# Rebuilt doors and attention in a two-layer trunk, with one of four weight homes given to the modulation

## The chip, the cores and the metric

The kernel runs on one core of a Trainium2 chip. The metric is the device time of one execution in microseconds (us); lower is better.

## What is computed

The reference is a decoder trunk of two layers on 256 rows of 2048 channels, all in float32. Each layer has a mixer and a feed-forward part (FFN), and both are wrapped in the same way:

```
mod = silu(c) @ w_ada[layer] + b_ada[layer]          # 6 x 2048 values: shift, scale, gate, twice
h = rmsnorm(x, g_pre) * (1 + sc) + sh
y = mixer(h)      # layer 0: gated MLP beside RWKV-7, one output projection; layer 1: attention
x = x + gt * rmsnorm(y, g_post)
h = rmsnorm(x, g_pre_ffn) * (1 + sc_f) + sh_f
gate, up = split(h @ w_ffn_in)                        # 2048 x 11264
x = x + gt_f * rmsnorm((silu(gate) * up) @ w_ffn_out, g_post_ffn)     # 5632 x 2048
```

With 256 rows the attention has a single key block, so each head is plain causal attention with a linear bias. The matrix `w_ada` is multiplied by one vector only.

## The kernel before

**Dense products.** `dense` computes 256 x 512 outputs: two row tiles of 128 (t = 0, 1), each summed in one PSUM bank `mm`. The weight comes in chunks of 2 x 128 rows by 512 columns, 512 KB each. `load_split` has SyncE (SP) load a chunk into a home `w32` (four of them in a ring, L193), ScalarE (ACT) round it to `wh` (L197) and VectorE (DVE) compute the rest `wl = w32 - wh` (L198); `wh` and `wl` have three buffers each. The activations are split in the same way into a high and a low part (`Ht`, `Lt`; named `hF`, `hFl` in the FFNs, `hA`, `hAl` in attention, `aH`, `aL` behind the gate). `mm_chunk` makes three products of 512 columns for each k tile and row tile (L209 high by `wh`, L210 high by `wl`, L211 low by `wh`), so 12 matmuls a chunk.

**Modulation.** The 320 blocks of `w_ada` that are worked off in the background are loaded by SP too (L150), 512 KB each, into homes of the tag `ada`, of which there are two. VectorE multiplies a block by the vector and sums it (L112), a "dot". Thirty-two dots make one of the ten vectors (0,2) to (1,5), finished at L136 to L143 (`mod`). After each chunk `pump` adds a rate to a credit and calls `ada_step` for each whole point: it issues a load and, as soon as as many are under way as there are homes, the dot of the oldest one.

**Order.** The program is written as one sequence and ordered by the framework's scheduler, per engine; `load_split` runs at a raised priority. Each engine works in order, and a waiting instruction holds up those behind it. SP's loads wait for a free home: a `w32` is free after its `wl`, an `ada` home after its dot.

**The doors.** Three times `residual_norm` leads from one part to the next: from layer 0's mixer to its FFN (door 1), from there to attention (door 2), from attention to layer 1's FFN (door 3). The last block of the part before is evacuated by `post_evac` (L261 `U`, L269 a sum, ACT squares), then the row sums are reduced (L284) and `X` is renewed block by block (L310, 512 columns and one row tile each). `X` is transposed by TensorE (L319), the second norm's factor is spread over all partitions by a small matmul (L327) and copied by ACT (L329); `h32` (tile `scr`, L338) multiplies transposed rows from PSUM by the scale and that factor, ACT adds the shift for `Ht` (L340), and VectorE gives `Lt` (L341). The scratch tiles take both homes of `ada`, after `ada_drain` has finished the dots under way.

**Attention.** Four groups of four heads. The three dense blocks of a group give k, q and v; k and q are copied (`znq`, L1152), transposed (L1159) and copied back. A generator (`Bg`) puts the heads of the group before between the chunks: scores (L1176, L1177), scale and bias, maximum, exponential, division (`pm`, L1190), transposes of `pm` (L1193), `pT`, and the product with v (L1199, L1200). Between these steps lie YA1, YA2 and YA3 points of credit, one point a chunk.

## Time and profile before

| what | us |
|---|---|
| median of three runs (lowest, highest) | 2522.0 (2519.48, 2523.02) |
| profiled execution, its span | 2523.41, 2521.7 |
| busy: TensorE | 2382.6 (94%) |
| busy: VectorE | 1668.5 (66%) |
| busy: ScalarE | 1078.7 (43%) |
| bytes loaded | 619.46 MB, 246 GB/s over the span |

The profile describes one execution; all its times count from the start of the span. "Busy" is time with an instruction under way on the engine; matmuls are pipelined, so a TensorE that is fed a little late still reads as busy. "PEclk" is the clock that TensorE was granted, as a share of 2.4 GHz.

By the trace the program runs so: start-up, gated MLP and RWKV to 553 us, the first FFN to 1337, attention with its output projection to 1752, the second FFN to 2511, the end of the output at 2521.7.

### The profile page before, as it was taken

The page shows a single profiled execution, that of the slowest core. Times are in us where ns is not written, and L with a number is a line of the kernel's source. Part 1 is how long each engine was busy: PE and PEld are TensorE (multiplying, and loading weights), DVE is VectorE, ACT ScalarE, POOL GpSimd, SP SyncE. Part 2 cuts the span into 40 slices and gives each one's busy share as a digit, 9 for nine tenths or more (in the row PEclk, how much of TensorE's full clock was granted, in tenths as well). Part 3 has the DMA queues.
Part 4 walks back from the last instruction along what each step waited for, and adds up shares of the span by engine and source line. Part 5 has one row for each costly group of instructions (what it writes and reads, how often), then busy time and mean ns, then how long its engine had stood idle before and what let it go on. Part 6 is the DMA issues. An engine that isn't in the chain of part 4 may idle for free. (4 is left out here: it accounts for less than half of the span.)

```text
span 2521.7 us, 30836 instructions
## 1 busy us (share of the span) xinstructions
PE 2382.6 (94%) x11536; PEld 1936.7 (77%) x11536; DVE 1668.5 (66%) x2267; ACT 1078.7 (43%) x1460; POOL 43.0 (2%) x30
## 2 busy tenths in 40 slices
PE   5898989978999999999998999999999999999998
PEld 4777877757877777888887777877777888888886
DVE  6759966888777777444447788876775544544444
ACT  2153444454444334444444444455444444444443
POOL 0001000000000000000000000100000000000000
PEclk9998989998999999999999999999999999999999
DMA  9975847786888888555555888975686555555554
GB/s 395 415 263 173 302 168 251 262 288 222 309 305 313 305 303 305 196 204 192 192 192 200 294 309 306 322 270 193 225 313 221 191 189 188 191 187 206 192 192 151
DMA packets 166566, 623.63 MB, mean 247 GB/s; under 512 B 18576, under 2 KB 18768, under 8 KB 161424
## 3 DMA queue, kind: packets, MB, share of 16 engines
q1 hardware_dynamic: 164256, 612.73, 69.0%
q10 hardware_dynamic: 2160, 8.94, 1.0%
q8 instruction: 90, 1.47, 0.2%
q14 instruction: 60, 0.49, 0.1%
HBM read 619.46 MB, written 2.13 MB: 246 GB/s over the span
## 5 line engine op out<-in xcount | busy, mean ns | idle before, releaser
L197 ACT ACTIVATE wh<-w 128x1024 fp32r<-128x1024 f32 x736 | 779.5, 1060 | 1087.1 <-PE mm L211 969.2
L198 DVE TENSOR_TENSOR wl<-w,wh 128x1024 fp32r<-128x1024 f32 x736 | 895.0, 1223 | 523.7 <-ACT wh L197 522.8
L210 PE MATMUL mm<-wl,hF 128*128 128x512 f32 x1408 | 554.8, 394 | 19.5 <-DVE wl L198 19.0
L209 PE MATMUL mm<-wh,hF 128*128 128x512 f32 x1408 | 553.4, 393 | 0.8 <-ACT hF L340 0.8
L211 PE MATMUL mm<-wh,hFl 128*128 128x512 f32 x1408 | 550.0, 391 | 0.0
L112 DVE SCALAR_TENSOR_TENSOR ada<-ada,cond 128x1024 f32<-128x1024 f32 x320 | 391.0, 1223 | 223.9 <-DMA ada<-in_w_ada_dram 222.3
L210 PEld LDWEIGHTS mm<-wl,hF 128*128 128x128 f32 x1408 | 264.8, 188 | 90.8 <-DVE wl L198 37.7
L209 PEld LDWEIGHTS mm<-wh,hF 128*128 128x128 f32 x1408 | 264.8, 188 | 55.4 <-ACT hF L340 1.0
L211 PEld LDWEIGHTS mm<-wh,hFl 128*128 128x128 f32 x1408 | 264.7, 188 | 54.0 <-DVE hFl L341 0.2
L211 PE MATMUL mm<-wh,aL 128*128 128x512 f32 x704 | 277.5, 394 | 0.0
L210 PE MATMUL mm<-wl,aH 128*128 128x512 f32 x704 | 276.1, 392 | 0.0
L209 PE MATMUL mm<-wh,aH 128*128 128x512 f32 x704 | 273.2, 388 | 0.0
L209 PE MATMUL mm<-wh,hA 128*128 128x512 f32 x384 | 156.1, 407 | 0.8 <-ACT hA L340 0.8
L210 PEld LDWEIGHTS mm<-wl,aH 128*128 128x128 f32 x704 | 132.1, 188 | 30.9
L209 PEld LDWEIGHTS mm<-wh,aH 128*128 128x128 f32 x704 | 132.2, 188 | 29.5
L210 PE MATMUL mm<-wl,hA 128*128 128x512 f32 x384 | 152.1, 396 | 1.4 <-DVE wl L198 1.4
L211 PEld LDWEIGHTS mm<-wh,aL 128*128 128x128 f32 x704 | 132.4, 188 | 26.2
L211 PE MATMUL mm<-wh,hAl 128*128 128x512 f32 x384 | 151.2, 394 | 0.0
L210 PEld LDWEIGHTS mm<-wl,hA 128*128 128x128 f32 x384 | 73.1, 190 | 16.3 <-DVE wl L198 2.3
L211 PEld LDWEIGHTS mm<-wh,hAl 128*128 128x128 f32 x384 | 72.9, 190 | 15.7 <-DVE hAl L341 0.2
L209 PEld LDWEIGHTS mm<-wh,hA 128*128 128x128 f32 x384 | 72.9, 190 | 15.5 <-ACT hA L340 1.1
L210 PE MATMUL mm<-wl,XH 128*128 128x512 f32 x128 | 52.8, 412 | 3.3 <-DVE wl L198 3.3
(315 smaller groups left out, 2346.8 us busy)
## 6 DMA issues: line engine op xcount, KB each, us to landing
w<-in_w_ffn_in_dram SPq DMA_DIRECT2D x352, 512.0 KB, 4.2
ada<-in_w_ada_dram SPq DMA_DIRECT2D x320, 512.0 KB, 5.2
w<-in_w_ffn_out_dram SPq DMA_DIRECT2D x176, 512.0 KB, 4.3
w<-in_w_qkv_dram SPq DMA_DIRECT2D x96, 512.0 KB, 4.9
w<-in_w_in_dram SPq DMA_DIRECT2D x56, 512.0 KB, 4.9
w<-in_w_out_dram SPq DMA_DIRECT2D x32, 512.0 KB, 4.6
w<-in_w_o_dram SPq DMA_DIRECT2D x32, 512.0 KB, 4.2
KB<-in_w_ada_dram SPq DMA_DIRECT2D x14, 1024.0 KB, 14.4
```

What stands on the lines that cost most here:

```text
L112: V.scalar_tensor_tensor(w, w, 1.0, cond[:, k0:k0 + n], op0=OP.mult, op1=OP.mult, accum_out=dst)
L197: A.activation(wh[:, :, :ncol], w32[:, :, :ncol], AF.Copy)
L198: V.tensor_sub(wl[:, :, :ncol], w32[:, :, :ncol], wh[:, :, :ncol].bitcast(F32))
L209: T.matmul(o, h, wh[:, k, :ncol], start=(kt == 0), stop=False)
L210: T.matmul(o, h, wl[:, k, :ncol], start=False, stop=False)
L211: T.matmul(o, l, wh[:, k, :ncol], start=False, stop=(kt == nkt - 1))
```

## The change

One of the four `w32` homes is given up for a third home of `ada`, both of 4 KB a partition. The rate at which dots are taken in the RWKV stage from its merges on rises from 1.7 to 2.4 a chunk. At the doors ACT multiplies the rows by the second norm's factor (`xr`) ahead of the transposes, so that the spreading matmul and its copy go; `Ht` comes from PSUM by one ACT operation, `h32` by a tensor_scalar, and `Lt` by one subtraction for two k tiles. The splits of the next part's first three chunks are issued from inside the door (`Pre`). The last block before a door, and the last of all, is `tail`: its last two chunks are taken for row tile 0 first and then for row tile 1. In attention the transposes of `znq` go through `Late` to behind the third chunk of the next block (`Late.at` is 2), and the steps of a head are written as functions, the scores of the next head standing ahead of the division of this one. `U` and the halves of attention's activations move to other tiles. The core of the diff (left out are the same functions' new names and pools):

```
-ADAB = 2
+ADAB = 3
...
-    def load_split(src, ncol):
-        w32 = wpool.tile([P, 2, 512], F32, tag="w32", name="w32", bufs=4)
+    class Pre:
+
+        q = []
+
+    def load_split(src, ncol, pri=PRI):
+        w32 = wpool.tile([P, 2, 512], F32, tag="w32", name="w32", bufs=3)
...
-        with tc.high_priority(PRI):
+        with tc.high_priority(pri):
...
-    def mm_chunk(ps, ch, wh, wl, xh, xl, ncol, nkt):
-        kts = [(k, t) for k in range(2) for t in range(NT)]
+    def mm_chunk(ps, ch, wh, wl, xh, xl, ncol, nkt, ts=range(NT)):
+        kts = [(k, t) for k in range(2) for t in ts]
...
-        for ch in range(nkt // 2):
-            wh, wl = load_split(wsrc(ch), ncol)
-            mm_chunk(ps, ch, wh, wl, xh, xl, ncol, nkt)
+        nch = nkt // 2
+        for ch in range(nch):
+            wh, wl = Pre.q.pop(0) if Pre.q else load_split(wsrc(ch), ncol)
+            if tail and ch == nch - 2:
+                held = wh, wl
+            elif tail and ch == nch - 1:
+                for t in range(NT):
+                    for c_, w_ in ((ch - 1, held), (ch, (wh, wl))):
+                        mm_chunk(ps, c_, *w_, xh, xl, ncol, nkt, (t,))
+            else:
+                mm_chunk(ps, ch, wh, wl, xh, xl, ncol, nkt)
...
         ada_drain()
-        scr = [wpool.tile([P, 4, S], F32, tag="ada", name="scr", bufs=ADAB) for _ in range(2)]
+        Pre.q = [load_split(src(0), 512)]
+        xr, hs = (wpool.tile([P, 4, S], F32, tag="ada", name="scr", bufs=ADAB) for _ in range(2))
...
-        def tr(k2):
...
-                    T.transpose(psv[:, k, tsl(t)], X[:, t, kt * P:(kt + 1) * P], ident)
...
+        def turn(qq):
+
+            qs = slice(qq * 512, (qq + 1) * 512)
+            for t in range(NT):
+                A.activation(xr[:, t, :], X[:, t, qs], AF.Copy, scale=r2[:, t:t + 1])
...
+                        T.transpose(banks[k2][:, k, tsl(t)], xr[:, t, f * P:(f + 1) * P], ident)
...
-            T.matmul(pb[:, tsl(t)], r2[:, t:t + 1].to_broadcast([P, P]), ident, start=True,
-                     stop=True)
-        A.activation(r2bc, pb[:, :S], AF.Copy)
...
-                V.scalar_tensor_tensor(h32, banks[k2][:, k, :], sc[:, kt:kt + 1], r2bc,
-                                       op0=OP.mult, op1=OP.mult)
-                A.activation(Ht[:, kt, :], h32, AF.Identity, bias=sh[:, kt:kt + 1])
-                V.scalar_tensor_tensor(Lt[:, kt, :], h32, sh[:, kt:kt + 1],
-                                       Ht[:, kt, :].bitcast(F32), op0=OP.add, op1=OP.subtract)
+                A.activation(Ht[:, kt, :], banks[k2][:, k, :], AF.Identity, bias=sh[:, kt:kt + 1],
+                             scale=sc[:, kt:kt + 1])
+                V.tensor_scalar(h32[:, k, :], banks[k2][:, k, :], sc[:, kt:kt + 1],
+                                sh[:, kt:kt + 1], op0=OP.mult, op1=OP.add)
+            ks = slice(2 * k2, 2 * k2 + 2)
+            V.tensor_sub(Lt[:, ks, :], h32, Ht[:, ks, :].bitcast(F32))
+            if k2 < 2:
+                Pre.q.append(load_split(src(k2 + 1), 512, 0))
+            if k2 in (1, 3, 5):
+                turn((k2 + 1) // 2)
...
-    RATE = (4.5, 2.0, 1.0, 1.7, 1.5)
+    RATE = (4.5, 2.0, 1.0, 2.4, 1.5)
...
+            Late.q.append(turn)
...
+        fr = [attn_front(4 * grp, 0, qT, kT)]
+        yield 1.5
         for i in range(4):
...
+            if i < 3:
+                fr.append(attn_front(4 * grp + i + 1, i + 1, qT, kT))
+            attn_norm(*fr[i])
             yield YA1
...
+            pT = attn_turn(*fr[i])
             yield YA2
...
+            attn_out(4 * grp + i, i, pT, vN)
```

The order on VectorE at door 1, before; `YP` is `U`, L261 and L269 are the end of `post_evac`, `mod_0_4` is the scale that the door needs:

```order
L112 SCALAR_TENSOR_TENSOR ada_3933,part_3546<-ada_3933,cond_72 128x1024
L269 SCALAR_TENSOR_TENSOR mm_3953,stm_3576<-YP_3009,SCN_102 128x512
L284 TENSOR_REDUCE tot_4047<-stm_3576 128x8
L278 RECIPROCAL r_post_4049<-r_post_4049 128x2
L310 SCALAR_TENSOR_TENSOR X_4040<-YP_3009,r_post_4049,SCN_102 128x512 x3
L112 SCALAR_TENSOR_TENSOR ada_3936,part_3546<-ada_3936,cond_72 128x1024
L278 RECIPROCAL r_pre_4057<-r_pre_4057 128x2
L310 SCALAR_TENSOR_TENSOR X_4040<-YP_3009,r_post_4049,SCN_102 128x512
L112 SCALAR_TENSOR_TENSOR ada_3939,part_3546<-ada_3939,cond_72 128x1024
L310 SCALAR_TENSOR_TENSOR X_4040<-YP_3009,r_post_4049,SCN_102 128x512 x3
...
L140 SCALAR_TENSOR_TENSOR mod_0_4_3948<-mod_0_4_3948,cols_70 128x16
L338 SCALAR_TENSOR_TENSOR scr_4045<-ms_4062,mod_0_4_3948,scr_4045 128x256 x2
```

After, the same place (L273 and L281 are the new numbers of L261 and L269, L296 and L290 of the reduce and its reciprocal, L324 of `X`, L351 of `h32`, L354 of `Lt`, L202 of `wl`; L213 to L215 are those of the three dense products):

```order
L202 TENSOR_TENSOR wl_4117<-w32_4114,wh_4116 128x1024
L273 TENSOR_TENSOR RA_99<-YP_3053,vA_103 128x512
L202 TENSOR_TENSOR wl_4128<-w32_4125,wh_4127 128x1024
L281 SCALAR_TENSOR_TENSOR mm_3980,stm_3653<-RA_99,SCN_102 128x512
L296 TENSOR_REDUCE tot_4080<-stm_3653 128x8
L290 RECIPROCAL r_post_4082<-r_post_4082 128x2
L324 SCALAR_TENSOR_TENSOR X_4067<-RA_99,r_post_4082,SCN_102 128x512 x3
L341 RECIPROCAL r_pre_4090<-r_pre_4090 128x2
L324 SCALAR_TENSOR_TENSOR X_4067<-RA_99,r_post_4082,SCN_102 128x512 x4
L351 TENSOR_SCALAR scr_4079<-ms_4097,mod_0_4_3742,mod_0_3_3249 128x256
...
L351 TENSOR_SCALAR scr_4079<-ms_4097,mod_0_4_3742,mod_0_3_3249 128x256
L354 TENSOR_TENSOR hFl0_4069<-scr_4079,hF0_4068 128x512
```

The dots between the rows of the door are gone from there, as are the last steps of `mod_0_4`, which are finished long before; two more `wl` stand in it.

The order on TensorE for one head of attention, before; between the scores and the transposes of `pm` stand 32 dense matmuls, here marked by "...":

```order
L1176 MATMUL ms_10309<-kT_9779,qT_9780 128x128
L1177 MATMUL ms_10309<-kT_9779,qT_9780 128x256
L209 MATMUL mm_10284<-wh_10323,hA_9656 128x512
...
L1193 MATMUL ms_10362<-cst_79,pm_10312 128x128 x3
L211 MATMUL mm_10284<-wh_10370,hAl_9657 128x512
...
L1199 MATMUL ms_10389<-pT_10366,vN_9781 128x256
L1200 MATMUL ms_10389<-pT_10366,vN_9781 128x128
```

After, for the same head and with the next one's scores (L1201 and L1202 the scores, L1217 the transposes, L1225 and L1226 the product with v):

```order
L1201 MATMUL ms_10330<-kT_9819,qT_9820 128x128
L1202 MATMUL ms_10330<-kT_9819,qT_9820 128x256
...
L1201 MATMUL ms_10364<-kT_9819,qT_9820 128x128
L1202 MATMUL ms_10364<-kT_9819,qT_9820 128x256
...
L1217 MATMUL ms_10438<-cst_79,pm_10333 128x128 x3
L213 MATMUL mm_10305<-wh_10446,hA_9681 128x512
...
L1225 MATMUL ms_10483<-pT_10442,vN_9821 128x256
L1226 MATMUL ms_10483<-pT_10442,vN_9821 128x128
```

The scores of two heads now stand together ahead, and 48 dense matmuls lie between the first head's scores and its transposes; 24 lie between those and the product with v, where there were four.

The order on SP in the first FFN, before. A `w32` waits for the `wl` of the chunk four before it in the ring, an `ada` for the dot two before:

```order
L193 DMA w32_5373<-in_w_ffn_in_dram 128x1024
L193 DMA w32_5401<-in_w_ffn_in_dram 128x1024
L150 DMA ada_6249<-in_w_ada_dram 128x1024
L193 DMA w32_5419<-in_w_ffn_in_dram 128x1024
L150 DMA ada_6306<-in_w_ada_dram 128x1024
L193 DMA w32_5440<-in_w_ffn_in_dram 128x1024
```

After, at a like place; a `w32` waits for the `wl` of the chunk three before it, an `ada` for the dot three before:

```order
L197 DMA w32_5441<-in_w_ffn_in_dram 128x1024
L197 DMA w32_5462<-in_w_ffn_in_dram 128x1024
L150 DMA ada_6439<-in_w_ada_dram 128x1024
L197 DMA w32_5480<-in_w_ffn_in_dram 128x1024
L150 DMA ada_6478<-in_w_ada_dram 128x1024
L197 DMA w32_5498<-in_w_ffn_in_dram 128x1024
```

The pattern of the two kinds of load stays; what moved is what each waits for. On VectorE the dot of `ada_6306` stands between the `wl` of `w32_5373` and that of `w32_5401`, both loaded before it, and the dot of `ada_6439` directly ahead of the `wl` of `w32_5462`, the load in front of it.

## Rows read from the trace of the kernel before

**Rows 1.** The page, chain that ended last: shares of the span by line.
```profile
PE mm L211 10%; PE mm L210 10%; PE mm L209 9%; DMA ada<-in_w_ada_dram 5%; DVE wl L198 1%; DVE ada L112 1%; PE ms L1107 0%; DVE X L310 0%; DVE X L1250 0%; PE ms L1199 0%; ACT wh L197 0%; SPq L193 0%; PE ms L1193 0%; PE ms L1177 0%; DVE scr L338 0%
```

**Rows 2.** Waits of TensorE, whole run: line, waited for, us in total, times, longest.
```profile
PE mm L210 <- DVE wl L198: 27.9, 39, 2.4
PE ms L319 <- DVE X L310: 22.8, 3, 12.6
...
PE ms L1193 <- DVE pm L1190: 7.3, 3, 3.6
...
PE ms L1159 <- ACT znq L1152: 4.4, 3, 2.6
```

**Rows 3.** Windows of tile w: us, busy (x count) of PE, PEld, DVE, ACT; PEclk, DMA, GB/s.
```profile
600.00:1000.00 400.00, 0.00 (x0) 0.00 (x0) 161.93 (x135) 144.56 (x137) 1.00 0.88 310
...
1800.00:1950.00 150.00, 0.00 (x0) 0.00 (x0) 62.31 (x53) 54.29 (x52) 1.00 0.79 275
1950.00:2250.00 300.00, 0.00 (x0) 0.00 (x0) 132.13 (x109) 114.56 (x108) 1.00 0.54 189
```

**Rows 4.** Waits of VectorE, 600 to 1000 us: us in total, times, longest.
```profile
DVE ada L112 <- DMA ada<-in_w_ada_dram: 97.2, 85, 3.4
```

**Rows 5.** Timeline of TensorE, 552.5 to 579 us: start, us, instruction.
```profile
552.84 0.39 PE L211 MATMUL mm<-wh,YB 128*128 128x512 f32 x1
...
578.87 0.63 PE L211 MATMUL mm<-wh,hFl 128*128 128x512 f32 x1
```

**Rows 6.** Timeline of VectorE, 552.5 to 577 us.
```profile
575.89 0.17 DVE L140 SCALAR_TENSOR_TENSOR mod<-mod,cols 128x16 f32<-128x16 f32 x1
576.18 1.27 DVE L338 SCALAR_TENSOR_TENSOR scr<-ms,mod,scr 128x256 f32<-128x256 f32 x3
```

**Rows 7.** Timeline of VectorE, 1336.5 to 1351 us.
```profile
1338.36 0.68 DVE L261 TENSOR_TENSOR YF<-mm,gtg 128x512 f32<-128x512 f32 x1
...
1340.83 0.18 DVE L284 TENSOR_REDUCE tot<-stf 128x8 f32<-128x32 f32 x1
...
1346.27 1.26 DVE L338 SCALAR_TENSOR_TENSOR scr<-ms,mod,scr 128x256 f32<-128x256 f32 x3
1347.45 0.74 DVE L310 SCALAR_TENSOR_TENSOR X<-YF,r_post,X 128x512 f32<-128x512 f32 x1
```

**Rows 8.** Timeline of TensorE, 1336.5 to 1351 us.
```profile
1336.82 0.40 PE L211 MATMUL mm<-wh,aL 128*128 128x512 f32 x1
...
1349.82 0.70 PE L211 MATMUL mm<-wh,hAl 128*128 128x512 f32 x2
```

**Rows 9.** Windows, all tiles, 577.8 to 583 us: PE, PEld, DVE, ACT, POOL; PEclk.
```profile
577.80:583.00 5.20, 5.20 (x17) 4.11 (x17) 5.20 (x13) 1.51 (x4) 0.00 (x0) 0.51 0.11 46
```

**Rows 10.** Waits of TensorE, 500 to 600 us.
```profile
PE mm L210 <- DVE wl L198: 5.4, 5, 2.4
```

**Rows 11.** Waits of VectorE, 450 to 553 us.
```profile
DVE ada L112 <- DMA ada<-in_w_ada_dram: 11.3, 12, 1.8
```

**Rows 12.** Timeline of TensorE in attention, 1435 and 1664 us.
```profile
1435.68 0.63 PE L210 MATMUL mm<-wl,hA 128*128 128x512 f32 x1
...
1664.65 0.82 PE L1193 MATMUL ms<-cst,pm 128*128 128x128 f32 x3 [2.31 <-DVE pm L1190]
```

**Rows 13.** Lines, 600 to 1000 us (busy, mean ns); tile w, 640 to 960 us.
```profile
L198 DVE TENSOR_TENSOR wl<-w,wh 128x1024 fp32r<-128x1024 f32 x135 | 162.1, 1220 | 3.6 <-ACT wh L197 3.6
L197 ACT ACTIVATE wh<-w 128x1024 fp32r<-128x1024 f32 x137 | 145.5, 1062 | 229.7 <-PE mm L211 195.4 <-DMA w<-in_w_ffn_in_dram 13.4 <-DVE ada L112 13.1
L112 DVE SCALAR_TENSOR_TENSOR ada<-ada,cond 128x1024 f32<-128x1024 f32 x100 | 122.5, 1225 | 98.1 <-DMA ada<-in_w_ada_dram 97.2
...
L193 SPq DMA_DIRECT2D w<-in_w_ffn_in_dram x107: 327/328/774, 643.3 to 957.9; - x107
...
DMA to landing us min/median/max: 3.4/5.3/7.9
```

**Rows 14.** Timeline of VectorE, the last 13 us.
```profile
2515.07 2.74 DVE L1250 SCALAR_TENSOR_TENSOR X<-YF,r,X 128x512 f32<-128x512 f32 x4
```

More of the change, by code (lines that the diff above doesn't have):

```diff
@@ L316, in tr @@
+        x_new(0)
+        V.reciprocal(r2, r2)
+        turn(0)
+        for k2 in range(KT // 2):
+            if k2 == 0 or k2 in (3, 5):
+                x_new((k2 + 1) // 2 + (k2 == 0))
+            h32 = hs[:, 2 * (k2 % 2):2 * (k2 % 2) + 2, :]
             for k in range(2):
                 kt = 2 * k2 + k
-                for t in range(NT):
-                    T.transpose(psv[:, k, tsl(t)], X[:, t, kt * P:(kt + 1) * P], ident)
-            banks[k2] = psv
-        x_new(0)
-        for k2 in range(2):
-            tr(k2)
@@ L933, in dense_T @@
         for ch in range(KT // 2):
-            w = wpool.tile([P, 2, 512], F32, tag="w32", name="w32", bufs=4)
+            w = wpool.tile([P, 2, 512], F32, tag="w32", name="w32", bufs=3)
             SY.dma_start(w, wsrc(ch))
@@ L1073, in trunk @@
         dense(lambda ch, b=b: wout[b, 4 + ch], 8, *hl(YB[:, 0], YB[:, 1]), 512, evac_yb(b),
[L1074 removed]
+              1, quiet=4 if b == 3 else 0, tail=b == 3)
         if b == 2:
@@ L1167, in evac_v, with attn_front @@
         return f
+    rg = (slice(0, 128), slice(128, 384))
+    def attn_front(h, i, qT, kT):
+        slope = 2.0 ** (-8.0 * (h + 1) / 16)
+        dh = qp.tile([P, 384], F32, tag="dh", name="dh", bufs=2)
+        G.tensor_scalar(dh, alibi, slope, None, op0=OP.mult)
+        sc = msbank()
+        T.matmul(sc[:, 0:128], qT[:, i, 0:128], kT[:, i, 0:128], start=True, stop=True)
+        T.matmul(sc[:, 128:384], qT[:, i, 128:256], kT[:, i, :], start=True, stop=True)
+        pm = qp.tile([P, 384], F32, tag="pm", name="pm", bufs=2)
+        V.scalar_tensor_tensor(pm, sc[:, 0:384], scale, dh, op0=OP.mult, op1=OP.add)
+        mx = small.tile([P, 2], F32, tag="mx", name="mx")
+        sm = small.tile([P, 2], F32, tag="sm", name="sm")
+        for t in range(NT):
+            V.tensor_reduce(mx[:, t:t + 1], pm[:, rg[t]], axis=AX.X, op=OP.max, negate=True)
+        for t in range(NT):
+            A.activation(pm[:, rg[t]], pm[:, rg[t]], AF.Exp, bias=mx[:, t:t + 1],
+                         accum_out=sm[:, t:t + 1])
+        return pm, sm
@@ new lines, in attn_turn, with attn_out @@
+    def attn_turn(pm, sm):
+        pt = msbank()
+        for j in range(3):
+            T.transpose(pt[:, j * P:(j + 1) * P], pm[:, j * P:(j + 1) * P], ident)
+        pT = qp.tile([P, 384], F32, tag="pT", name="pT", bufs=2)
+        A.activation(pT, pt[:, 0:384], AF.Copy)
+        return pT
+    def attn_out(h, i, pT, vN):
+        po = msbank()
+        vs = slice(i * P, (i + 1) * P)
+        T.matmul(po[:, 0:256], vN[:, 0, vs], pT[:, 0:256], start=True, stop=False)
+        T.matmul(po[:, 128:256], vN[:, 1, vs], pT[:, 256:384], start=False, stop=True)
+        split_from(po[:, 0:256], oH[:, h, :], oL[:, h, :])
@@ L1169, in attn_gen, with attn_norm @@
+    def attn_norm(pm, sm):
+        V.reciprocal(sm, sm)
+        for t in range(NT):
+            V.tensor_scalar(pm[:, rg[t]], pm[:, rg[t]], sm[:, t:t + 1], None, op0=OP.mult)
     def attn_gen(grp, qT, kT, vN):
+        fr = [attn_front(4 * grp, 0, qT, kT)]
+        yield 1.5
         for i in range(4):
-            h = 4 * grp + i
-            slope = 2.0 ** (-8.0 * (h + 1) / 16)
-            dh = tp_.tile([P, 384], F32, tag="dh", name="dh", bufs=2)
-            G.tensor_scalar(dh, alibi, slope, None, op0=OP.mult)
@@ L1175, in attn_gen @@
-            sc = msbank()
-            T.matmul(sc[:, 0:128], qT[:, i, 0:128], kT[:, i, 0:128], start=True, stop=True)
-            T.matmul(sc[:, 128:384], qT[:, i, 128:256], kT[:, i, :], start=True, stop=True)
-            pm = tp_.tile([P, 384], F32, tag="pm", name="pm", bufs=2)
-            V.scalar_tensor_tensor(pm, sc[:, 0:384], scale, dh, op0=OP.mult, op1=OP.add)
-            mx = small.tile([P, 2], F32, tag="mx", name="mx")
-            sm = small.tile([P, 2], F32, tag="sm", name="sm")
@@ L1191, in attn_gen @@
-            pt = msbank()
-            for j in range(3):
-                T.transpose(pt[:, j * P:(j + 1) * P], pm[:, j * P:(j + 1) * P], ident)
-            pT = tp_.tile([P, 384], F32, tag="pT", name="pT", bufs=2)
-            A.activation(pT, pt[:, 0:384], AF.Copy)
-            yield YA2
-            po = msbank()
-            vs = slice(i * P, (i + 1) * P)
-            T.matmul(po[:, 0:256], vN[:, 0, vs], pT[:, 0:256], start=True, stop=False)
-            T.matmul(po[:, 128:256], vN[:, 1, vs], pT[:, 256:384], start=False, stop=True)
```

102 lines of the change are left out of this document (48 added, 54 removed).

## Prediction

> **What bounds the kernel now.** I began with the chain that ended last: its largest shares are TensorE's and, behind it, that of transfers [rows 1]. TensorE is the bound, so the question is where it does not run at its own pace. The list of what TensorE waited for names four places that the change touches: the low weight parts `wl`, `X` at the three doors, `pm` and `znq` in attention [rows 2]. These waits add up to 62 us, 22.8 of them at the doors and 11.7 in attention.
>
> That list misses what pipelining hides, so I then counted `wl` tiles per stretch [rows 3]. In 1950 to 2250 us, where no modulation is loaded, there are 109 in 300 us: 2.752 us for a chunk of 12 matmuls, 0.229 each. That is TensorE's own pace. In 600 to 1000 us, where the modulation is loaded beside the weights, there are 135, and at most one more by its cut ends, so 136 in 400 us, 2.94 each: 136 x 0.188 = 25.6 us lost. In 1800 to 1950 us 53 tiles in 150 us make 2.83, a loss of 4 us. VectorE meanwhile stands before `ada` dots whose data have not landed, 97.2 us in 85 waits [rows 4], with the next weight's `wl` queued behind each. So in these stretches the loads' round trip sets the pace.
>
> **Door 1, after the RWKV stage.** The last matmul starts at 552.84 and the first product with a low part, L211, at 578.87 [rows 5]: 25.6 us behind its end (552.84 + 0.39). The trace of VectorE shows why: dots of the modulation (0,4) lie between the `X` blocks, and the first `h32` (L338) starts at 576.18, just behind the last step of that modulation at 575.89 [rows 6]. In the order after, all dots that the door needs are ahead of it. I add what is left, with the durations of door 2, where no such dots stand [rows 7]. From `U` of the second row tile (1338.36) to the reduce (1340.83) 2.47 us go by, one `wl` among them; door 1 has an addition of 0.64 and one more `wl` of 1.22 there, so 4.33. From the reduce to the first use of transposed banks 5.44 (1340.83 to 1346.27). Then L351, `X`, two L351 and the first L354: 0.42 + 0.74 + 0.84 + 0.64. The 0.42 is a third of L338's 1.26, also a product out of PSUM; for a tensor_scalar from PSUM no row exists, so 0.42 is the upper bound and half of `X`'s 0.74, 0.37, at half the elements, the lower. L354 has half the elements of a `wl` and is taken as half of it, as is the addition; both ends, 0.61 and 0.74, hardly differ. Sum 12.4; with a wait here or there I take 12.7. Door 1: **-13**, bounds -10 and -14.
>
> **Doors 2 and 3.** Before, 12.6 us lie between the last matmul's end (1336.82 + 0.40) and L211 at 1349.82 [rows 8]. After, by the same sum with one `wl`, 10.6, if the first row tile's part, which `tail` lets end 12 matmuls (2.7 us) before the end in place of 6, is through by then; 11.8 if its `wl` slips behind. Gain 0.8 to 2.0; I take 1.3. Against it stands the clock. Behind door 1's long wait the granted clock was 0.51, so 1.2 GHz, for the 5.2 us in which the dense matmuls began, and 17 matmuls were done where 5.2 / 0.229 = 22.7 fit at 2.4 GHz: 5.7 matmuls, 1.3 us lost [rows 9]. At doors 2 and 3 that stretch may now lie under the transposes, which nobody waits for. After, the transposes start later, behind ACT's scaling of the rows, and are sooner followed by dense matmuls, so I charge 1.3 at each. The Trainium skill, "TensorE: Matmul & The Clock Gate", section "HAM oscillation", says that gaps without TensorE work bring the slow clock back. The row of door 1 agrees in kind; by that rule alone, with every door's dense start slow, the same 1.3 would be charged, and without it the sum would be 2.6 us lower. Doors 2 and 3 net: **0**, bounds -2 and +2.5 each. The splits of the first three chunks, taken ahead of the door, remove part of the `wl` waits that follow it (5.4 us between 500 and 600 [rows 10]): **-2**, bounds 0 and -5.
>
> **Dots moved ahead of door 1.** By the order eight more dots stand ahead of it, 8 x 1.23 = 9.8 us of VectorE. Between 450 and 553 us VectorE idles 11.3 us in front of late `ada` data [rows 11], which a third home shortens. I take 0; without that cover it is +9.8.
>
> **Attention.** The scores of a head are issued a turn earlier; between them and the transposes of `pm` stand 48 dense matmuls in place of 32 to 36, so 11.0 us in place of 7.3 to 8.3; with the longest wait, 3.6 [rows 2], 10.9 to 11.9 were needed, so it just does. The transposes of `znq` move back into the next dense block, by 96 matmuls or more. Both kinds of wait go, 7.3 + 4.4, except that the last head has no dense work to hide behind: its 2.3 us stay [rows 12]. That is 9.4 us. Behind the wait of 3.6 dense matmuls take 0.63 where 0.39 is usual [rows 12, 5]: the slow clock; I charge 3 us in all for two such places, an estimate from the 1.3 of door 1. Attention: **-12**, bounds -7 and -15.
>
> **Homes: four of `w32` to three, two of `ada` to three.** The round of a weight's home is its landing 5.3, `wh` 1.06, `wl` 1.22 [rows 13], 7.58 us. Where a dot stands just ahead of that `wl`, its load is issued straight behind the weight's in SP's order: 0.33 for the issue, a landing like the weight's, 5.3, the dot 1.23 and `wl` 1.22, 8.08. With 100 dots to 136 weights the mean is 7.95. Three homes at TensorE's pace allow 3 x 2.752 = 8.26. It just fits, with 0.3 us over for the other work of VectorE and for landings that scatter from 3.4 to 7.9. The third `ada` home gives every such load a lead of three chunks where two or three were. Hence half of what is lost: **-13** in the first FFN (bounds 0 and -25.6, the slower case below), **-2** of 4 in the second.
>
> **End.** The first row tile's sums end 6 matmuls earlier, 1.4 us; the last `X` blocks start only when the first tile's are through (2515.07 [rows 14]): **-1**, bounds 0 and -1.4.
>
> Sum: -13 + 0 - 2 + 0 - 12 - 13 - 2 - 1 = -43. The profiled execution took 2523.4, so 2480.4; the median of the runs lies 1.4 lower: **2479**.
>
> **Rivals.**
> - *The third home does not do what it is there for.* SP issues in order; an `ada` load that could go out stands behind a weight load whose home is not free, so the dots wait as long as before. Both FFNs gain nothing: 2523.4 - 28 - 1.4 = **2494**. For it: with three homes each weight load, and the `ada` load behind it, waits on a `wl` one nearer. Against it: a freed `ada` home is waited for today as well.
> - *The FFNs run at TensorE's pace.* All 25.6 + 4 come back: 2523.4 - 28 - 29.6 - 1.4 = **2464**. For it: the 97.2 us of dots that wait [rows 4]; against it, a round that fits by 0.3 us only.
> - *Slower: three homes bind.* Today's pace is lost when the round passes 3 x 2.94 = 8.82, so when landing rises from 5.3 to 6.2. At 6.9 the round is 9.55 and a chunk 3.18; over the 136 and 53 chunks counted above that is 136 x 0.24 + 53 x 0.35 = 51 us more, and 2523.4 + 51 - 28 - 1.4 = **2545**. From a landing of 6.6 on it eats the 28 us of doors, attention and end. Against it: landings have their median at 5.3 with 310 GB/s, and the pace can rise by 7% at most. The Trainium skill, "DMA: Bandwidth & Descriptors", section "Latency and other measured facts", gives an HBM access 0.2 us on average and 2 us under high load; by that, 1.3 us more of landing would be possible, and this rival would hold. No row here shows such a step.
> - *The dots ahead of door 1 show*, and the FFNs gain nothing: 2494 + 10 = **2504**, up to 2511 where attention gains its lower bound.
>
> **How the numbers follow.** Forecast 0.46 (2467 to 2492), the home without use 0.23, TensorE's pace 0.15, the dots 0.07, slower 0.09. All but the last are faster by over 0.2% (5 us, about what a measurement of this kernel tells from no change), less a little for the ends of the last two: faster 0.88, within 0.03, slower 0.09. For 8 in 10 the range has to hold the home without use and most of TensorE's pace: 2453 to 2510.
>
> **What would show it.** In the profile after: the first product with a low part some 12.7 us behind the last matmul at door 1 and 10.6 to 12 at the others; waits of transposes on `pm` and `znq` gone but for one of some 2 us; 138 to 145 `wl` in 400 us of the first FFN; dots that wait on their transfers well under 97 us. I am wrong if landing passes 6.2 us, if waits on `wl` grow, or if the stage ahead of door 1 ends later than 553 by more than a few us.

## The result, and the profile after

The changed kernel takes 2487.2 us (four runs, 2484.12 to 2495.83) against 2520.74 before: a ratio of 0.9879, 95% interval 0.9861 to 0.9898, so 25 to 35 us faster. The prediction was 2479, 43 us faster. Its profiled execution took 2484.1, the fastest of the four, with this span and engines:

```profile
span 2482.4 us, 30655 instructions
...
PE 2363.4 (95%) x11524; PEld 1925.0 (78%) x11524; DVE 1669.8 (67%) x2243; ACT 1091.7 (44%) x1481; POOL 40.2 (2%) x30
```

What TensorE waited for over the whole run (line, waited for, us in total, times, longest):

```profile
PE mm L214 <- DVE wl L202: 26.9, 34, 2.8
PE ms L338 <- ACT scr L331: 22.6, 3, 8.2
...
PE mm L213 <- ACT wh L201: 5.5, 3, 4.4
...
PE ms L1217 <- DVE pm L1232: 0.2, 1, 0.2
```

Beside [rows 2]: the long waits on `pm` and `znq` are gone, and `wl` is waited for as long as before, 26.9 us for 27.9. The doors' wait (now L338, on ACT's scaled rows) is 22.6 for 22.8, three even waits in place of one of 12.6 and two of 5.

The `wl` count by stretch (as [rows 3]) and VectorE's waits in the first of them (as [rows 4]):

```profile
600.00:1000.00 400.00, 0.00 (x0) 0.00 (x0) 169.18 (x139) 146.75 (x139) 1.00 0.87 307
...
1800.00:1950.00 150.00, 0.00 (x0) 0.00 (x0) 65.86 (x54) 57.04 (x54) 1.00 0.71 241
1950.00:2250.00 300.00, 0.00 (x0) 0.00 (x0) 132.37 (x108) 113.75 (x108) 1.00 0.59 192
```

```profile
DVE ada L112 <- DMA ada<-in_w_ada_dram: 81.1, 79, 3.0
DVE wl L202 <- ACT wh L201: 15.5, 16, 1.5
```

139 tiles in 400 us make 2.88 us a chunk, where 2.94 stood and 2.75 is TensorE's own pace. The dots still wait 81 us for their data.

ScalarE's row shows what is new in that stretch: `wh` waits for its weight to land, 159.7 us in all, where [rows 13] had 13.4:

```profile
L201 ACT ACTIVATE wh<-w 128x1024 fp32r<-128x1024 f32 x139 | 147.6, 1062 | 237.4 <-DMA w<-in_w_ffn_in_dram 159.7 <-DVE ada L112 50.0 <-PE mm L215 13.5
```

Door 1 on TensorE (as [rows 5]); the dense matmuls begin at 556.91, 10.2 us behind the end of the last one, where it was 24.65:

```profile
546.37 0.39 PE L215 MATMUL mm<-wh,YB 128*128 128x512 f32 x1
554.95 2.16 PE L338 MATMUL ms<-cst,scr 128*128 128x128 f32 x8 [8.19 <-ACT scr L331]
556.91 0.79 PE L213 MATMUL mm<-wh,hF 128*128 128x512 f32 x1
```

Each program consists of the same 8640 dense matmuls, so the two traces can be laid side by side at the first and last matmul of each stage. All in us, from the profiled executions:

| stage | before | after | change | forecast |
|---|---|---|---|---|
| start to the first `YB` block | 503.58 | 490.19 | -13.4 | none |
| `YB` blocks, up to door 1 | 49.65 | 56.57 | +6.9 | 0 (bound +9.8) |
| door 1 | 24.65 | 10.15 | -14.5 | -13 |
| first FFN, input | 516.95 | 512.25 | -4.7 | -13, -2 behind the doors |
| first FFN, output | 242.55 | 242.55 | 0 | 0 |
| door 2 | 11.57 | 9.33 | -2.2 | -1.3 |
| attention and its output | 408.47 | 401.98 | -6.5 | -12 |
| door 3 | 11.29 | 9.05 | -2.2 | -1.3 |
| second FFN, input | 499.68 | 498.47 | -1.2 | -2 |
| end | 11.07 | 9.65 | -1.4 | -1 |

(The rest, 0.2 us a seam, is overlap of matmuls; the forecast of doors 2 and 3 had +1.3 each for the clock besides, which falls into the stage behind the door.) The doors' rows end at the first dense matmul, L213. The forecast counted to the first product with a low part, L215: by that measure door 1 went from 25.65 to 13.69 us, door 2 from 12.60 to 12.20 and door 3 from 12.33 to 12.59, so doors 2 and 3 gained next to nothing. The sum by the profiles is -39.3; the medians show -33.5. The runs of the changed kernel scatter by 12 us, and its profile is of the fastest of them, while that of the kernel before is of one of its slower ones.

The total was near, but two terms are far off, and 13.4 us come from a place that the forecast gave nothing. So the experiments ask for the cause of each: homes, doors, attention's order or the rate.

### The profile page after: what moved, and what is told of

It reads as the page before. It is cut to its first block, busy times and chain, and to the rows that moved or that the text cites. A ratio compares the mean times of both kernels' runs of the same rounds, so it can differ in the third digit from the quotient of the medians.

```text
span 2482.4 us, 30655 instructions
## 1 busy us (share of the span) xinstructions
PE 2363.4 (95%) x11524; PEld 1925.0 (78%) x11524; DVE 1669.8 (67%) x2243; ACT 1091.7 (44%) x1481; POOL 40.2 (2%) x30
## 4 chain that ended last, share of the span: by engine, by line
PE 53%; DMA 24%; DVE 14%; issue 6%; ACT 3%; SPq 1%; DVEq 0%; ACTq 0%
DMA ada<-in_w_ada_dram 17%; PE mm L214 16%; PE mm L215 16%; PE mm L213 16%; DVE wl L202 6%; DVE ada L112 2%; DMA RA<-in_w_lora_dram 2%; DMA w<-in_w_ffn_in_dram 2%; ACT wh L201 1%; DMA vA<-in_w_lora_dram 1%; SPq L197 1%; PE mm L491 1%; DMA w<-in_w_out_dram 1%; DMA w<-in_w_in_dram 1%; DMA KB<-in_w_ada_dram 0%
## 5 line engine op out<-in xcount | busy, mean ns | idle before, releaser
L202 DVE TENSOR_TENSOR wl<-w,wh 128x1024 fp32r<-128x1024 f32 x736 | 899.1, 1223 | 534.4 <-ACT wh L201 531.6
L214 PE MATMUL mm<-wl,hF 128*128 128x512 f32 x1408 | 553.4, 393 | 13.6 <-DVE wl L202 13.4
L213 PE MATMUL mm<-wh,hF 128*128 128x512 f32 x1408 | 553.2, 393 | 0.0
L215 PE MATMUL mm<-wh,hFl 128*128 128x512 f32 x1408 | 550.2, 391 | 0.0
L213 PEld LDWEIGHTS mm<-wh,hF 128*128 128x128 f32 x1408 | 264.9, 188 | 54.2 <-ACT hF L349 0.4
L215 PEld LDWEIGHTS mm<-wh,hFl 128*128 128x128 f32 x1408 | 264.6, 188 | 54.3
L215 PE MATMUL mm<-wh,aL 128*128 128x512 f32 x704 | 275.5, 391 | 0.0
L213 PE MATMUL mm<-wh,aH 128*128 128x512 f32 x704 | 274.6, 390 | 0.0
L213 PEld LDWEIGHTS mm<-wh,aH 128*128 128x128 f32 x704 | 132.2, 188 | 30.2
L213 PE MATMUL mm<-wh,hA 128*128 128x512 f32 x384 | 155.0, 405 | 0.0
L215 PEld LDWEIGHTS mm<-wh,aL 128*128 128x128 f32 x704 | 132.3, 188 | 27.8
L215 PE MATMUL mm<-wh,hAl 128*128 128x512 f32 x384 | 151.1, 393 | 0.0
L215 PEld LDWEIGHTS mm<-wh,hAl 128*128 128x128 f32 x384 | 72.1, 188 | 15.7 <-DVE hAl L354 0.3
L213 PEld LDWEIGHTS mm<-wh,hA 128*128 128x128 f32 x384 | 72.3, 188 | 14.4 <-ACT hA L349 0.2
```

The lines of the kernel that those rows point to most:

```text
L202: V.tensor_sub(wl[:, :, :ncol], w32[:, :, :ncol], wh[:, :, :ncol].bitcast(F32))
L213: T.matmul(o, h, wh[:, k, :ncol], start=(kt == 0), stop=False)
L214: T.matmul(o, h, wl[:, k, :ncol], start=False, stop=False)
L215: T.matmul(o, l, wh[:, k, :ncol], start=False, stop=(kt == nkt - 1))
```

## The experiments

Times are medians; each ratio is to runs of the kernel before that were taken beside it. The stages below come from each run's profiled execution, as above. The number of weight homes stands in two lines of the kernel, which differ alike; one is shown.

| kernel | us | ratio (95%) | first FFN starts | its input | attention | gaps at doors 2, 3 |
|---|---|---|---|---|---|---|
| before | 2518.4, 2516.9 | | 577.9 | 517.0 | 408.5 | 11.6, 11.3 |
| changed | 2487.2 | 0.9879 (0.9861, 0.9898) | 556.9 | 512.3 | 402.0 | 9.3, 9.1 |
| homes_back | 2518.4 | 1.0006 (0.9990, 1.0023) | 583.9 | 516.8 | 407.9 | 9.3, 9.1 |
| homes_alone | 2478.0 | 0.9850 (0.9824, 0.9876) | 554.6 | 510.2 | 398.1 | 11.6, 11.3 |
| w3a2 | 2515.6 | 0.9986 (0.9968, 1.0005) | 574.6 | 519.7 | 406.8 | 11.6, 11.3 |
| w2a4 | 2721.7 | 1.0799 (1.0770, 1.0828) | 576.5 | 558.6 | 459.7 | 14.0, 12.9 |
| rate_back | 2475.5 | 0.9829 (0.9805, 0.9853) | 543.6 | 514.6 | 408.4 | 9.3, 9.0 |
| old_attn | 2488.4 | 0.9876 (0.9849, 0.9903) | 560.2 | 505.7 | 401.3 | 9.3, 9.1 |
| rate_oldattn | 2472.0 | 0.9802 (0.9776, 0.9828) | 547.9 | 508.5 | 403.0 | 9.3, 9.1 |

**The homes as before, all else changed (homes_back).**

```diff
-ADAB = 3
+ADAB = 2
-        w32 = wpool.tile([P, 2, 512], F32, tag="w32", name="w32", bufs=3)
+        w32 = wpool.tile([P, 2, 512], F32, tag="w32", name="w32", bufs=4)
```

> The changed kernel with the homes as before: two of the modulation, four of the weights; doors, attention, tail and rate stay as changed. Theory 1 (the exchange of homes pays in the RWKV stage and a little in the FFNs, and costs in attention, where 8.0 us of waits on wl stand after the change): the 13.4 us that the RWKV stage has won go, the first FFN takes 517 us in place of 512, attention with its output projection about 8 us less than 402; in sum about 10 us slower than the changed kernel. Theory 2 (the exchange is worth nothing in the RWKV stage, that lead is the rate's): RWKV keeps its lead, attention wins 8, the FFNs lose 6; in sum the same as the changed kernel or a few us faster.

It takes 2518.4 us: without the exchanged homes nothing at all is left of the change. Theory 1 had the direction and a third of the size; its 8 us less in attention did not come (407.9 for 402.0). The new door is in it, and yet door 1 is longer than ever; TensorE's wait there, and VectorE's work ahead of the first `X` (L324):

```profile
PE ms L338 <- ACT scr L331: 24.3, 1, 24.3
```

```profile
554.12 0.17 DVE L140 SCALAR_TENSOR_TENSOR mod<-mod,cols 128x16 f32<-128x16 f32 x1
...
565.93 1.22 DVE L112 SCALAR_TENSOR_TENSOR ada<-ada,cond 128x1024 f32<-128x1024 f32 x1
...
567.85 1.22 DVE L112 SCALAR_TENSOR_TENSOR ada<-ada,cond 128x1024 f32<-128x1024 f32 x1
...
571.43 1.22 DVE L112 SCALAR_TENSOR_TENSOR ada<-ada,cond 128x1024 f32<-128x1024 f32 x1
...
574.73 1.23 DVE L112 SCALAR_TENSOR_TENSOR ada<-ada,cond 128x1024 f32<-128x1024 f32 x1 [2.08 <-DMA ada<-in_w_ada_dram]
...
575.88 1.41 DVE L324 SCALAR_TENSOR_TENSOR X<-RA,r_post,SCN 128x512 f32<-128x512 f32 x2
```

The vector (0,4) is finished at 554.12, before the last matmul (557.30 + 0.39). But the higher rate has ordered further dots ahead of the door, and with two homes they come one by one, one of them after 2.08 us of waiting for its load. The new door does not start until 575.88. What doors 2 and 3 and the end save is lost here. The rate of 2.4 stands in this kernel too; the other changes with the old homes and the old rate were not run.

**The homes alone (homes_alone).** The kernel before, with

```diff
-ADAB = 2
+ADAB = 3
-        w32 = wpool.tile([P, 2, 512], F32, tag="w32", name="w32", bufs=4)
+        w32 = wpool.tile([P, 2, 512], F32, tag="w32", name="w32", bufs=3)
```

> The kernel before with only the homes exchanged (three of the modulation, three of the weights); old doors, old attention, old rate. Theory 1: the RWKV stage is about 8 to 13 us shorter, the first FFN 5 us, attention longer by some us; 5 to 15 us faster than before. Theory 2: no change in the RWKV stage; within 5 us of before.

40 us faster than before: at least as much as the whole change. Theory 1 holds, with three times its size, except that attention got shorter and not longer (398.1 for 408.5). The old door passes in 13.3 us, 8.02 of them the wait for `X`, and the first product with a low part (L211) starts 14.5 us behind the end of the last matmul, where it was 25.6:

```profile
540.92 0.39 PE L211 MATMUL mm<-wh,YB 128*128 128x512 f32 x1
549.33 2.21 PE L319 MATMUL ms<-cst,X 128*128 128x128 f32 x8 [8.02 <-DVE X L310]
...
555.79 0.50 PE L211 MATMUL mm<-wh,hFl 128*128 128x512 f32 x1
```

The early part shows what the third home does. SP's wait for a free modulation home between 130 us and the dense blocks, before and with the homes alone:

```profile
SPq L150 <- DVE ada L112: 56.2, 16, 7.2
```

```profile
SPq L150 <- DVE ada L112: 36.5, 16, 6.4
```

SP works in order, so what it waits for an `ada` home also holds the loads behind it. Nine dots more are done when the `YA` blocks begin (72 for 63), eleven more when `YB` begins (89 for 78), so that all of (0,4) but seven dots is through: door 1 no longer meets them.

**One home fewer, and two exchanged (w3a2, w2a4).** Both start from the kernel before. In w3a2 `ADAB` stays 2; in w2a4 it is 4 and the other line ends with `bufs=2`:

```diff
-        w32 = wpool.tile([P, 2, 512], F32, tag="w32", name="w32", bufs=4)
+        w32 = wpool.tile([P, 2, 512], F32, tag="w32", name="w32", bufs=3)
```

> The kernel before with only one weight home taken away: three of the weights, two of the modulation. If a third modulation home is all of the gain and the weights' fourth home is idle store, this is the same as before (2518). If a fourth weight home was worth something, the first FFN, whose three-home round leaves 0.3 us, takes 520 us or more in place of 517 and attention 312 or more in place of 309: 5 to 20 us slower.

> The kernel before with two homes exchanged: two of the weights, four of the modulation. A round of a weight's home is 7.6 to 8.1 us, so two homes allow a chunk no faster than 3.8 us where TensorE needs 2.75: over the two FFN input stages of 176 chunks each some 300 us more, and the output stages (landing 4.3, round 6.6, chunk 3.3) 100 us more; 2800 to 2950 us. If landing shrinks as fewer loads are under way, to about 3.5 (round 5.8, chunk 2.9): 2530 to 2600.

With three of the weights and two of the modulation the time is that of before (0.9986), and so is the number of tiles in the first FFN:

```profile
600.00:1000.00 400.00, 0.00 (x0) 0.00 (x0) 164.19 (x135) 142.61 (x135) 1.00 0.87 308
```

So the fourth weight home was worth nothing where the modulation had two, and the gain of homes_alone is the third modulation home's. The queue's own waits do not say so: in the kernel before, between 640 and 960 us, SP stood longer before weight homes than before modulation homes:

```profile
SPq L193 <- DVE wl L198: 130.6, 79, 5.4
SPq L150 <- DVE ada L112: 56.3, 26, 3.8
```

Four beside three was not tried. There it might be worth something: with three of each, `wh` waits 159.7 us for its weights in the first FFN, as shown above. That stays open. With two of the weights the kernel is 8% slower, between the two expected cases. Landing of a weight there, and all engines, 640 to 960 us:

```profile
DMA to landing us min/median/max: 3.3/3.7/5.1
```

```profile
640.00:960.00 320.00, 301.83 (x1253) 223.86 (x1252) 239.73 (x319) 119.63 (x136) 0.00 (x0) 1.00 0.87 306
```

At 306 GB/s a weight lands in 3.7 us, where it took 5.3 before at 310 [rows 3, 13]. The time to landing follows the number of loads that are under way more than the rate. Counted in the traces at each issue between 640 and 960 us, a load with two, three and four others under way lands in 4.8, 5.7 and 6.6 us before (medians), one with one, two and three in 3.4, 4.0 and 5.0 us in w2a4.

**The old rate (rate_back).**

```diff
-    RATE = (4.5, 2.0, 1.0, 2.4, 1.5)
+    RATE = (4.5, 2.0, 1.0, 1.7, 1.5)
```

> The changed kernel with the rate of the RWKV stage from the merges on back at 1.7. If the rate moves the dots ahead of door 1 and does nothing else: the last quarter of the RWKV stage (YB blocks, 56.6 us after, 49.7 before) loses its 7 us, and the wait at door 1 takes them back: 8 more dots of 1.3 us, about 10 us, stand in the door; same as changed or up to 5 us slower. If the lead ahead of the merges is the rate's: 13 us slower.

The `YB` blocks lose more than their 7 us (44.7 for 56.6), door 1 does not take them back (9.9 for 10.2), and the median falls by 12 us to 2475.5. The dots in that stretch (each dot is two instructions; busy VectorE, clock, DMA share, GB/s), changed and with the old rate:

```profile
490.20:546.70 56.50, 20.70 (x34) 0.94 0.83 280
```

```profile
489.00:534.00 45.00, 10.86 (x18) 1.00 0.78 267
```

17 dots against 9: eight dots, 1.5 us each. They are neither needed at the door nor covered: VectorE is busy 51.3 of the stage's 56.6 us, and 42.8 of 44.7 with the old rate, so it is nearly full either way. old_attn and rate_oldattn, below, differ by the rate alone too and show the same, 56.9 and 45.8 us. Neither of the expected cases came: both had the kernel the same or slower.

**Attention's old order (old_attn, rate_oldattn).** Evacuation and heads as in the kernel before, with YA1, YA2, YA3 = 3, 1, 1; the second with the rate of 1.7 too. The core of the edit:

```diff
-YA1, YA2 = 3.5, 2
+YA1, YA2, YA3 = 3, 1, 1.0
...
-            Late.q.append(turn)
...
-        fr = [attn_front(4 * grp, 0, qT, kT)]
-        yield 1.5
         for i in range(4):
-            if i < 3:
-                fr.append(attn_front(4 * grp + i + 1, i + 1, qT, kT))
...
+            yield YA3
```

> The changed kernel with attention's old order (transposes of znq at once, scores, division, transposes and product of a head one after the other, 3, 1 and 1 points apart). If the loads set attention's pace with three homes, the waits on pm and znq come back but lie in part beside the loads' round: the two stages of attention together 402 us after, 408 before, here 404 to 408. If the new order is worth its waits, 9 to 12 us: 411 to 414.

> The changed kernel with the old rate of 1.7 and attention's old order: what is left of the change is the homes, the new doors with their early splits, and the tail. If the new order of attention is worth nothing, 2475 like the kernel with the old rate alone, or a few us under it; if it is worth its 9 us of waits, 2484. Against the homes alone (2478) the doors, 3.4 + 2.2 + 2.2 by gaps, and the end, 1.5, should show as 9 us less: 2469.

The time is the same with either order: 2488.4 for 2487.2 at the new rate, 2472.0 for 2475.5 at the old one, intervals overlapping; attention takes 401.3 and 403.0 us with the old order, 402.0 and 408.4 with the new one. What TensorE waits for differs: with the old order (rate_oldattn) for `pm` and `znq` (L1213, L1179), with the new one for `wl`, here with the old rate and in the changed kernel:

```profile
PE ms L1213 <- DVE pm L1210: 4.2, 3, 1.8
PE ms L1179 <- ACT znq L1172: 0.9, 1, 0.9
PE mm L214 <- DVE wl L202: 0.2, 1, 0.2
```

```profile
PE mm L214 <- DVE wl L202: 10.1, 11, 2.6
```

```profile
PE mm L214 <- DVE wl L202: 8.0, 9, 1.6
```

With the new order and the old homes (homes_back) it is `wl` as well, so the third home is not its cause:

```profile
PE mm L214 <- DVE wl L202: 10.1, 10, 3.1
```

**Attention without loads of the modulation (nodots_new; left_new, left_old).** All three have the old rate of 1.7. In nodots_new the qkv blocks have a rate of their own; in left_new and left_old the list of the vectors is cut (and `need` takes the bias for those left out):

```diff
-            dense(lambda ch, j=j: wqkv[3 * grp + j, ch], KT, hx, lx, 512, ev, 0.65 if grp or j else 0.0, 1.0)
+            dense(lambda ch, j=j: wqkv[3 * grp + j, ch], KT, hx, lx, 512, ev, 0.0, 1.0)
```

```diff
-    ada_order = [(0, 2), (0, 3), (0, 4), (0, 5), (1, 0), (1, 1), (1, 2), (1, 3), (1, 4), (1, 5)]
+    ada_order = [(0, 2), (0, 3), (0, 4), (0, 5), (1, 0), (1, 1)]
```

> The changed kernel with the old rate and no dots in the qkv stage of attention (they are moved behind it, so only that stage's length is read): new order of the heads. If loads of the modulation beside the weights set that stage's pace, it falls from 307 us to 295 or less, and TensorE waits for neither pm, znq nor wl there. If TensorE sets it, it stays at 305 or more.

> The changed kernel with the old rate and attention's new order; it leaves out the modulation vectors (1,2) to (1,5), 128 of the 320 blocks with their loads and dots (the bias stands for them), so that attention and the second FFN run without them. If those loads set the pace of attention, its qkv stage falls from 306 us to 290 or less, without waits on wl; the second FFN's input falls from 498 to 491 us, what 176 chunks at 2.75 and its transposes take.

> The same with attention's old order. If the new order is worth its waits as soon as loads do not hide them, the qkv stage here is 9 to 12 us longer than with the new order, and TensorE waits for pm and znq; if the order is worth nothing in any case, within 2 us.

The first says nothing: the scheduler put the dots into that stage all the same, 81 of them (two instructions each) in its 300 us, where the changed kernel has 80:

```profile
1320.00:1620.00 300.00, 98.32 (x162) 0.99 0.87 302
```

The two that leave blocks out, in one execution each, do: the qkv stage falls from 308.6 (rate_back) to 294.8 us with the new order and from 304.1 (rate_oldattn) to 296.4 with the old one, though not to the 290 expected. No wait on `wl` is left with either, and with the old order none on `pm` or `znq` either; the list for that stretch holds only the door:

```profile
PE ms L342 <- ACT scr L335: 7.4, 1, 7.4
```

The second FFN's input falls to 494.1 and 493.5 us, less far than the 491 expected.

**Parts of the door (notail, nopre).** Both from rate_oldattn; in notail the four calls lose `tail=b == 3`, in nopre these lines go:

```diff
-        Pre.q = [load_split(src(0), 512)]
...
-            if k2 < 2:
-                Pre.q.append(load_split(src(k2 + 1), 512, 0))
```

> The changed kernel with the old rate, attention's old order and no tail: the last two chunks of a block before a door in the order of before. If the doors' shorter gaps (9.3 and 9.1 us in place of 11.6 and 11.3) are the tail's, they return to 10.5 or more; the end, 9.6 us behind the last matmul, returns to 11.1 in any case.

> The changed kernel with the old rate, attention's old order and no early splits (the first three chunks are split in the next block, as before). If the early splits hold the door's own work on VectorE up, the gaps at doors 2 and 3 get 1 to 2 us shorter than 9.3 and 9.1 and the first chunks wait on wl instead; if they cost nothing, the gaps stay and the 12 chunks behind a door take up to 2 us longer.

Single executions, 2477.1 and 2464.0 us, which the scatter does not tell apart. The gaps do: without `tail` 9.27 and 9.03 at doors 2 and 3, without the early splits 9.32 and 9.05, both as with them; so neither of these makes the gap, and what is left for it are the door's new steps, which were not taken apart. The 12 chunks behind doors 2 and 3 end no later without the early splits (48.8 and 46.9 us behind the last matmul for 49.0 and 47.0), and behind door 1 TensorE waits 0.2 us for `wl` with them and without, so the early splits show no gain. `tail` shows at door 1 (10.28 for 9.93) and at the end (10.95 for 9.60).

## Why the prediction was right, and where it was not

**Total.** The direction and the range held. The likeliest case was too good by 8 us. That it came so near is in part luck. 28 of its 43 us were to come from the doors with their splits, attention and the end, yet with the old homes none of the change's gain is left (homes_back); the stages from which it took a gain gave 32.7 us, some 10 less than forecast, and 13.4 us from the start, which is in no term, less 6.9 for the dots, made up for more than half of that.

**Homes.** The step that failed most is the one that gave the exchange 15 us and looked for it in the FFNs alone. By homes_alone and w3a2 it is the whole gain of some 40 us: 23 us up to the start of the first FFN (11 of them at door 1), 7 in its input, 10 in attention (1.7 of them in w3a2 too); 2.6 us in the second FFN are no more than w3a2 shows too. In the first FFN the round was sized at 7.95 us, so that it "just fits" the 8.26 of TensorE's pace, and this failed: followed through the trace, a weight takes 8.76 us on average from its issue to the end of its `wl` (109 loads between 640 and 960 us), which is the pace, 3 x 2.88 = 8.6. The landing of weights stayed much the same (5.1 for 5.3), that of `ada` rose from 5.4 to 6.0; minimum, median and longest, first for weights and for `ada` in the changed kernel, then for `ada` before:

```profile
DMA to landing us min/median/max: 3.3/5.1/7.7
```

```profile
DMA to landing us min/median/max: 4.3/6.0/8.6
```

```profile
DMA to landing us min/median/max: 4.2/5.4/7.4
```

With three `ada` homes a load is issued earlier and lands later. The dots wait 81 us in place of 97, and `wl` now waits for `wh` (15.5 us in place of 3.6), which fits a load that is issued one `wl` later. The case of "no use" was wrong, that of full pace too; half was too much by a factor of two or so. "Dots well under 97 us" did not come either, with 81. The rival in which three homes bind did not come as slower time, since the weights' median landing did not rise to 6.2; but `wh` now waits for its weights, which suggests that three homes hold the pace at 2.88. Four beside three of the modulation would show it, and was not run.

**Door 1.** The size was nearly right: to the first product with a low part 12.0 us less, 13.69 for 12.7 expected, and 14.5 less to the first dense matmul; the cause that the text gave, dots that stand in the door, was right too. What takes them away is the third home, not the new order: with the old door and the homes alone the gap is 13.3, with the new door and the old homes 26.2, and with the old door, the old rate and a weight home fewer (w3a2) 25.3. The new door's own share is 13.3 - 9.9 = 3.4 us (homes_alone against rate_back).

**Dots ahead of door 1.** Taken as covered; the bound of +9.8 was the truth. Measured: 12 us in the `YB` blocks for eight dots (rate_back). The cover named was VectorE's idle time in front of late data; with the third home it is mostly gone (5.7 us are left between 450 and 547 us of the changed kernel, 1.6 of them in the `YB` blocks), so it could cover little. Less than half of it, 5.1 us, had stood in the `YB` blocks before.

**Start to `YB`.** Not in the sum; the argument had not looked ahead of 450 us, where SP stood 56 of 141 us before an `ada` home. With three such homes the first dense block starts at 262.7 to 266.8 us in ten kernels, with two at 267.1 to 271.0 in three: some 5 us on average are the third home's. The rest of the 13.4 stays open: the four dense blocks that follow take 162.4 us before and 156.3 after, but 155.9 to 165.3 among the kernels with the third home, and 157.1, 161.6 and 155.9 in three that are the same up to there (rate_oldattn, notail, nopre), so it lies within the scatter.

**Attention.** Forecast -12, measured -6.5, and not by the step that was named. The waits on `pm` and `znq` were taken for a matter of distance: 7.3 and 4.4 us that 48 matmuls would cover. They did go, but the qkv stage, where all but one stood, got only 2.1 us shorter (308.8 to 306.6). left_old shows why: with the old distances and no modulation, TensorE waits for neither. What was late was VectorE, held by dots and their loads (which of the two is not separated); with the new order the lateness shows at `wl`. Without modulation the stage takes 294.8 (new order, and 1.6 more at its end) and 296.4 (old). With it, three homes and the new order the qkv stage takes 306.6 to 309.3 us in three profiles, with the old order 301.8 to 307.2 in five; with two homes 312.7 and 308.8 to 309.6. So the new order gains nothing, and rather loses a few us where the modulation is loaded; the medians do not tell the two apart. On average the third home is worth some 4 us of the stage in either order.

The rest of the 6.5 us lies behind it: the output projection takes 93.7 us for 99.4, less 1.3 more between the two stages. It holds seven dots before and none after. Among the kernels with three or four weight homes, all with the rate of 2.4 have none there and take 93.6 to 95.0 us, those with 1.7 and the whole modulation five to seven dots and 96.0 to 99.4. So this part is the rate's: of the dots taken ahead of door 1, where they cost 12 us, this stage is spared.

**Doors 2 and 3.** Forecast net nothing, with 1.3 saved and 1.3 given back to the clock. Measured: the gap to the first dense matmul is 2.2 shorter, that to the first product with a low part 0.4 shorter at door 2 and 0.3 longer at door 3. Twelve chunks behind door 2 TensorE stands 47.8 us behind the last matmul before it, for 48.4 before; at door 3 47.6 for 47.6. So the saving is given back, and the granted clock shows part of it, 1320.9 to 1325 after and 1348.8 to 1353 before, each the first 4 us of dense work (the last three columns: clock, DMA share, GB/s):

```profile
1320.90:1325.00 4.10, 4.08 (x20) 3.03 (x20) 4.07 (x7) 4.10 (x9) 0.00 (x0) 0.81 0.00 0
```

```profile
1348.80:1353.00 4.20, 4.20 (x22) 3.40 (x23) 4.20 (x12) 2.66 (x6) 0.00 (x0) 1.00 0.37 125
```

0.81 in place of 1.00 over 4.1 us is 0.8 us. Before, the slow clock, 0.50 or 1.2 GHz, lay under the transposes, here for 5 us behind the wait; after, it reaches into the dense work, which begins at 1320.88:

```profile
1342.40:1347.40 5.00, 4.94 (x21) 4.14 (x22) 5.00 (x10) 1.07 (x4) 0.00 (x0) 0.50 0.52 191
```

```profile
1318.90:1322.30 3.40, 3.38 (x14) 2.50 (x14) 3.29 (x6) 2.62 (x6) 0.00 (x0) 0.50 0.14 57
```

So the charge for the clock was right in kind. The first transposes before, and the transposes and the first dense matmuls after:

```profile
1342.37 2.20 PE L319 MATMUL ms<-cst,X 128*128 128x128 f32 x8 [5.15 <-DVE X L310]
```


```profile
1311.16 0.40 PE L215 MATMUL mm<-wh,aL 128*128 128x512 f32 x1
1318.92 2.16 PE L338 MATMUL ms<-cst,scr 128*128 128x128 f32 x8 [7.37 <-ACT scr L331]
1320.88 0.80 PE L213 MATMUL mm<-wh,hA 128*128 128x512 f32 x1
...
1323.75 0.50 PE L215 MATMUL mm<-wh,hAl 128*128 128x512 f32 x1
```

TensorE waits 7.37 us where it waited 5.15, and the clock is at 0.50 behind either wait; what differs is that 20 transposes and the four spreading matmuls stood ahead of the dense work before, and eight transposes after. By the Trainium skill, "TensorE: Matmul & The Clock Gate", section "HAM oscillation", gaps without TensorE work bring the slow clock back, and the rows of both kernels agree. The door's steps on VectorE:

```profile
1315.22 0.17 DVE L296 TENSOR_REDUCE tot<-stf 128x8 f32<-128x32 f32 x1
...
1320.86 0.54 DVE L351 TENSOR_SCALAR scr<-ms,mod,mod 128x256 f32<-128x256 f32 x1
1321.32 0.74 DVE L324 SCALAR_TENSOR_TENSOR X<-YF,r_post,X 128x512 f32<-128x512 f32 x1
1321.98 0.99 DVE L351 TENSOR_SCALAR scr<-ms,mod,mod 128x256 f32<-128x256 f32 x2
1323.01 0.69 DVE L354 TENSOR_TENSOR hAl<-scr,hA 128x512 fp32r<-128x512 f32 x1
```

From the reduce to the first L351 it takes 5.64 us, for 5.44 in the sum; the first tensor_scalar out of PSUM 0.54, for 0.42 as upper bound, since a third of three overlapping L338 is less than one alone; L354 0.69 for 0.64. The sum also began at `U` of the second row tile and left out what lies between the last matmul and `U`, 1.14 us before (1336.82 + 0.40 to 1338.36 [rows 7, 8]). The 10.6 to 11.8 became 12.2 (1311.16 + 0.40 to 1323.75).

**Splits ahead of the doors.** Forecast -2. By nopre they show nothing: the `wl` waits that were counted for them lay mostly in the `YB` blocks, ahead of door 1 (1.2 of the 5.4 us [rows 10] are behind it).

**End.** Forecast -1, measured -1.4; by notail it is the tail's.

## What to carry to other kernels

Where several streams of loads share one queue that works in order, count for each stream how long the engine that uses its data waits for them to land, and try a buffer less for the stream that comes in time and one more for the stream that is late. Before, between 600 and 1000 us, `wh` waited 13.4 us for its weights and the dots 97.2 for theirs. How long the queue stands before a stream's buffers does not tell it: between 640 and 960 us SP stood 130.6 us before weight homes and 56.3 before modulation homes, and the fourth weight home was still worth nothing (w3a2). The gain then appears wherever that stream was late, not only where it was looked for. A wait that a trace names (a transpose on `pm`) can be only the last link: test whether it goes when the load behind it is left out before reordering around it. And a merged change should be taken apart: here one edit of two numbers is nearly all the gain, the doors and the end are worth a few us by the gaps (the medians, 2472.0 for 2478.0, do not tell them apart), attention's order nothing, one edit (the rate) costs 12 us, and taking that one back, with attention's old order, gives the fastest of the complete kernels that ran several times: 2472.0 us, 0.9802 (0.9776 to 0.9828).
